# Projections, Fourier blocks and memory attention in phases, the later phases issued one unit behind

## The chip, the cores and the metric

The kernel runs on one core of a Trainium2 chip. The metric is the device time of one execution in microseconds; lower is better. The kernel before was timed three times: 2253.23, 2254.17 and 2257.09 us, median 2254.17.

The core has five engines, each with its own in-order instruction queue: TensorE (PE in the profile; PEld are its weight loads), VectorE (DVE), ScalarE (ACT), GpSimd (POOL) and SyncE (SP), which issues most of the DMAs. An engine waits on semaphores that the others raise.

## The reference

A two-layer encoder on a sequence of 1024 tokens of width 1024. In each layer, cut to the mixing part:

```python
h = _rmsnorm(x, g_pre_mix[l])
z = h @ w_in[l]
zf, zq, zk, zv, zm = jnp.split(z, splits, axis=-1)      # 256, 512, 128, 128, 256
y_f = _fourier_mix(zf, w_fourier[l])                    # FFT over tokens and channels, real part, then 64x64 maps
q, k = _rope(zq), _rope(zk)                             # 8 query heads, 2 key heads of 64
y_a = _window_attn(q, k, zv, sink[l])                   # keys within 128 tokens, one sink per head
y_m = _memory_attn(zm, km, vm)                          # 4 heads over 256 memory rows
y = concat([_rmsnorm(y_f), _rmsnorm(y_a), _rmsnorm(y_m)]) @ w_out[l]
x = x + _rmsnorm(y, g_post_mix[l])
```

A SwiGLU feed-forward block with width 2816 follows, again with a norm before and behind it. Everything is float32.

## The kernel before

Products run on TensorE in pairs of float32r halves: `split` (line 149) makes of an array a high half (an ACT cast, line 151) and the difference to it, the low half (line 152, on DVE, or on POOL where the caller says so). `Acc.add` (line 162) then issues three matmuls per block of 128 rows: high x high, high x low, low x high.

The 1024 tokens are eight tiles of 128. Per layer the mixing part does, in program order:

- `zf` (line 488): the projection for the Fourier group and its channel transform, by halves of the sequence; its results are the tiles `PQ`.
- `fourier_units` (line 509): one unit `even`, then four `e_out`, then `odd`, then four `o_out`. `even` and `odd` are long sums on DVE (line 512 in the profile). Each `e_out` and `o_out` ends in `finish`: load a table of cosines (`c_dft`), split it and the data, 6 products into a PSUM tile `yfp`, square and scale on ACT (lines 545 and 547, with a small POOL chain between), two transposes `yfT` on TensorE, two copies.
- `kvz` (line 625), one unit per token tile: 24 matmuls of 512 columns into `kvp` (keys, values, memory queries), then the readers of that PSUM tile: the split of the values, an ACT copy of the memory queries (line 639), and `rope` on the keys (DVE lines 612 and 614, then a POOL sum at line 617), then transposes `zT` (line 643) and `kT` (line 648) in the same unit.
- `q` (line 659): 24 matmuls into `qp`, `rope` (lines 612, 614, 617), four transposes `qT` (line 666), two stacks of halves. `q_load` fetches and splits the weights (eight 256 KB loads, `load_w512`, line 342, low halves on POOL). The weights of `kvz` and `q` share one pool of four buffers, `big`.
- `mem_units` (line 812): unit i does `mem_values` of pair i - 1 (transposes `mpT`, splits, products `mav`) and then `mem_scores` of pair i (products `ms`, maximum, exponential, scaling on POOL at line 790).
- `att_units` and `fm_units`: window attention and the output projection.

`weave` (line 59) merges two lists of units evenly in program order. The tile framework then decides the order on each engine from the program order, the dependences and its own timeline, so what runs next to what is read from the order lists below. PSUM has four pools of two banks: `sc`, `pT`, `av` and `pd` (line 42). `qp`, `qT` and `kvp` take `pd`; `kT` and `mav` take `av`. SBUF buffers are rings in two arenas (lines 125 to 136): a ring hands its places out in turn, and a place is written again only when its last reader is through.

## Time and profile before

| | |
|---|---|
| Median of three runs | 2254.17 us |
| The profiled execution's own time | 2256.81 us |
| Its span on the core, which the profile covers | 2255.0 us |
| Mean granted TensorE clock | 0.964 |
| TensorE busy | 2084.4 us |
| VectorE busy | 1495.7 us |
| ScalarE busy | 1078.5 us |
| GpSimd busy | 612.6 us |

A row of a table of stretches gives, for one stretch of the span, its length, the busy time of each engine with the number of instructions, the granted TensorE clock as a share of full speed, the mean busy share of the DMA engines and the rate. A row in order of time gives start, length, engine, line, operation, output<-input, shapes and count; in brackets stands how long the engine sat idle before it and which instruction it then waited for. The length of a row of several matmuls covers all of them. A row of a group gives the count, then busy time and mean of one in ns, then idle time before and its releasers.

### The profile page before, as it was taken

Reading aid. Unit: us, or ns where it says so; the run is one execution under the profiler, and the core shown is the slowest. Engines: PE = TensorE matmul, PEld = TensorE weight load, DVE = VectorE, ACT = ScalarE, POOL = GpSimd, SP = SyncE. Lnnn points to the kernel's source line nnn. Section 1 sums busy time; section 2 is a strip of 40 time slices with the busy share of each in tenths; the row PEclk is TensorE's granted clock in tenths of the full one; section 3 lists DMA queues with packets and bytes.
Section 4 is the critical chain, followed back from the end, with each engine's and each line's share of the span. In section 5 each row is a group of like instructions: output and inputs, shape, how many; then the busy total and the mean of one; then the engine's idle time right before and its main releaser. Section 6 shows DMA issues by size and latency. Waiting matters only on the chain.

```text
span 2255.0 us, 27659 instructions
## 1 busy us (share of the span) xinstructions
PE 2084.4 (92%) x9538; PEld 1703.3 (76%) x9538; DVE 1495.7 (66%) x2370; ACT 1078.5 (48%) x2179; POOL 612.6 (27%) x681
## 2 busy tenths in 40 slices
PE   7988898689999999999998789986999999999997
PEld 6767686568888887888886567765788888888876
DVE  7545878787676765565755478787867676644555
ACT  6354867553333334443544468675433333333343
POOL 5142425332222223210102334353522222200110
PEclk9989999889999999999998899998999999999999
DMA  6110322413222226666631112233222222255765
GB/s 212 33 54 2 101 86 84 140 47 103 75 94 75 94 71 197 220 194 209 221 117 33 40 43 75 76 122 112 75 76 93 75 94 75 91 182 169 239 206 177
DMA packets 135581, 252.85 MB, mean 112 GB/s; under 512 B 11256, under 2 KB 86032, under 8 KB 135440
## 3 DMA queue, kind: packets, MB, share of 16 engines
q1 hardware_dynamic: 129680, 240.59, 32.2%
q10 hardware_dynamic: 5760, 10.49, 1.2%
q8 instruction: 75, 1.23, 0.2%
q14 instruction: 66, 0.54, 0.1%
HBM read 201.76 MB, written 49.28 MB: 111 GB/s over the span
## 4 chain that ended last, share of the span: by engine, by line
PE 63%; DVE 6%; POOL 3%; issue 3%; ACT 3%; DMA 2%; DVEq 0%; SPq 0%; POOLq 0%; ACTq 0%
PE fo L1126 19%; PE qz L1026 10%; PE qx L1026 10%; PE qy L1026 10%; PE qw L1026 5%; PE mo L162 3%; DVE arena_r L152 2%; PE qp L162 2%; PE kvp L162 1%; PE zT L162 1%; POOL big L980 1%; DMA arena_f<-in_w_ffn_out 1%; DVE arena_f L1016 1%; ACT arena_r L151 1%; PE av L728 1%
## 5 line engine op out<-in xcount | busy, mean ns | idle before, releaser
L151 ACT CAST arena_r<-arena_f 128x512 fp32r<-128x512 f32 (+3 forms) x702 | 449.8, 660 | 774.4 <-PE fo L1126 181.6
L152 DVE TENSOR_TENSOR arena_r<-arena_f,arena_r 128x512 fp32r<-128x512 f32 (+4 forms) x678 | 571.6, 852 | 329.6 <-ACT arena_r L151 320.2
L1126 PE MATMUL fo<-arena_r 128*128 128x512 f32 x2112 | 491.4, 393 | 8.8 <-ACT arena_r L151 4.0
L1126 PEld LDWEIGHTS fo<-arena_r 128*128 128x128 f32 x2112 | 397.5, 189 | 95.6 <-ACT arena_r L151 5.9
L1026 PE MATMUL qy<-arena_r 128*128 128x512 f32 x1056 | 259.9, 396 | 15.6 <-ACT arena_r L151 9.6
L1026 PEld LDWEIGHTS qy<-arena_r 128*128 128x128 f32 x1056 | 201.4, 191 | 60.0 <-ACT arena_r L151 10.8
L1026 PE MATMUL qz<-arena_r 128*128 128x512 f32 x704 | 196.6, 390 | 4.5 <-ACT arena_r L151 1.9
L1016 DVE TENSOR_TENSOR arena_f<-arena_f 128x512 f32<-128x512 f32 x220 | 192.4, 878 | 11.2 <-DMA arena_f<-in_w_ffn_in 5.8
L1049 POOL TENSOR_TENSOR arena_f<-arena_f 128x512 f32<-128x512 f32 x44 | 76.0, 1728 | 423.0 <-ACT arena_f L1031 423.0
L1026 PEld LDWEIGHTS qz<-arena_r 128*128 128x128 f32 x704 | 132.1, 188 | 33.5 <-ACT arena_r L151 2.7
L1026 PE MATMUL qx<-big,arena_r 128*128 128x512 f32 x528 | 128.8, 393 | 2.5 <-DVE big L152 2.1
L208 POOL TENSOR_SCALAR rrsv<-rss 128x1 f32<-128x1 f32 x32 | 11.0, 342 | 442.2 <-ACT arena_f L320 225.7
L1026 PE MATMUL qw<-arena_r 128*128 128x512 f32 x528 | 129.1, 392 | 1.9 <-DVE arena_r L152 1.9
L1026 PE MATMUL qx<-arena_r 128*128 128x512 f32 x528 | 128.6, 393 | 1.7 <-DVE arena_r L152 1.7
L1078 POOL TENSOR_TENSOR arena_f<-arena_f 128x512 f32<-128x512 f32 x44 | 71.7, 1630 | 183.4 <-DVE arena_f L1059 104.5
L1026 PEld LDWEIGHTS qx<-big,arena_r 128*128 128x128 f32 x528 | 100.1, 190 | 24.6 <-DVE big L152 2.9
L1026 PEld LDWEIGHTS qx<-arena_r 128*128 128x128 f32 x528 | 100.4, 190 | 23.1 <-DVE arena_r L152 2.0
L1026 PEld LDWEIGHTS qw<-arena_r 128*128 128x128 f32 x528 | 99.8, 189 | 23.5 <-DVE arena_r L152 2.7
L1026 PE MATMUL qz<-big,arena_r 128*128 128x512 f32 x352 | 115.2, 389 | 0.0
L162 PE MATMUL qp<-big,arena_r 128*128 128x512 f32 x384 | 107.6, 433 | 3.1 <-POOL big L152 2.4
L162 PE MATMUL mo<-arena_r 128*128 128x512 f32 x384 | 105.0, 420 | 3.0 <-ACT arena_r L151 3.0
L162 PE MATMUL mo<-big,arena_r 128*128 128x512 f32 x384 | 101.1, 402 | 1.9 <-ACT arena_r L151 1.2
(197 smaller groups left out, 3225.5 us busy)
## 6 DMA issues: line engine op xcount, KB each, us to landing
arena_f<-in_w_ffn_out SPq DMA_DIRECT2D x132, 512.0 KB, 3.6
arena_f<-in_w_ffn_in SPq DMA_DIRECT2D x88, 512.0 KB, 3.5
actd<-arena_f SPq DMA_DIRECT2D x44, 512.0 KB, 2.6
arena_f<-actd SPq DMA_DIRECT2D x88, 192.0 KB, 2.8
arena_f<-in_w_in SPq DMA_DIRECT2D x40, 256.0 KB, 2.8
arena_f<-in_x SPq DMA_DIRECT2D x16, 512.0 KB, 4.3
arena_f<-in_w_out SPq DMA_DIRECT2D x32, 256.0 KB, 2.7
pmd<-arena_f ACTq DMA_DIRECT2D x32, 256.0 KB, 2.0
```

What stands on the lines that cost most here:

```text
L151: nc.scalar.copy(hi, src)
L152: return (lo_eng or nc.vector).tensor_tensor(out=lo, in0=src, in1=f32(hi), op=ALU.subtract)
L162: mm(self.dst, a, b, start=self.i == 0, stop=self.i == self.n - 1)
L208: nc.gpsimd.tensor_scalar(out=v, in0=ss, scalar1=1.0 / n, scalar2=EPS, op0=ALU.mult, op1=ALU.add)
L728: mm(av, lhs, p_, start=j == 0 and i == 0, stop=j == nk - 1 and i == 1)
L980: nc.gpsimd.tensor_tensor(out=b21, in0=b21, in1=b22, op=ALU.add)
L1016: nc.vector.tensor_tensor(out=s, in0=a, in1=b, op=op)
L1026: mm(pt, a, b, start=start and n == 0, stop=n == 11, skip_group_check=not start)
L1049: nc.gpsimd.tensor_tensor(out=self.v, in0=self.v, in1=self.s2, op=ALU.add)
L1078: (nc.gpsimd if i in (0, 3) else nc.vector).tensor_tensor(out=a[:, 512 * (i % 2) : 512 * (i % 2) + 512], in0=c, in1=g[i], op=ALU.mult)
L1126: mm(pts[t][m], a[:, x, sl], w[y][:, ns], start=ff == 0 and j == 0, stop=ff == NFF - 1 and j == 2)
```

## The change

- `finish` is cut into `halves` (table load and splits), `products` (the six products, square, scale) and `turned` (transposes and copies). Unit i does `halves` of block i, `products` of block i - 1, `turned` of block i - 2. `odd` moves into unit 1.
- `kvz` first copies the whole PSUM tile to SBUF with one ACT instruction (ring `kvs` of three); values, `rope` and memory queries read that copy, and the values' low half is made on POOL. Its transposes become `kvz_turn`, called one unit behind by the new helper `skewed`.
- `q` keeps products and `rope`; the transposes become `q_turn`, one unit behind, and `qT` moves from the PSUM pool `pd` to `av`. The ring for query `rope` has six places instead of four, elsewhere in the arena.
- `mem_values` is cut into `mem_turn` (transposes and splits) and `mem_values` (products); unit i does scores of pair i, values of pair i - 2, transposes of pair i - 1.
- `load_w512` makes low halves in turn on DVE and POOL instead of on POOL alone. The ring `tabs` has four places instead of two.
- `q_load` stands before the last unit of `kvz_turn`; `fm_load` moves into the weave of the memory units, after the last query products.

```diff
-    ropes = {2: run(6, 4, 0.5), 8: run(8, 4, 2)}
+    ropes = {2: run(6, 4, 0.5), 8: run(36, 6, 2)}
...
-            split(hi, lo, raw, nc.gpsimd)
+            split(hi, lo, raw, (nc.vector, nc.gpsimd)[k % 2])
...
+            order = (0, 4, 2, 6, 1, 5, 3, 7)
+
+            def unit(i):
+                if i == 1:
+                    odd()
+                if i < 8:
+                    (e_out if order[i] % 2 == 0 else o_out)(order[i])
+                if 1 <= i < 9:
+                    products(order[i - 1])
+                if i >= 2:
+                    turned(order[i - 2])
+
+            return [even] + [lambda i=i: unit(i) for i in range(10)]
...
             wmov(self.wkvz, self.hT, t, pt)
+            r = kvs(512)
+            nc.scalar.copy(r, pt)
             vst = self.vst[half][:, c]
-            split(vst[:, :, 0, :], vst[:, :, 1, :], pt[:, P : 2 * P].rearrange("p (g d) -> p g d", g=2))
-            z = zs_(256)
-            nc.scalar.copy(z, pt[:, 2 * P : 4 * P])
-            kr = self.rope(pt[:, 0:P], 2, t)
+            split(vst[:, :, 0, :], vst[:, :, 1, :], r[:, P : 2 * P].rearrange("p (g d) -> p g d", g=2), nc.gpsimd)
+            self.kvr[t] = self.rope(r[:, 0:P], 2, t), r[:, 2 * P : 4 * P]
+
+        def kvz_turn(self, t):
+            half, c = divmod(t, 4)
+            kr, z = self.kvr.pop(t)
             zt = ps([2, P], "zT", "pT")
...
+        def skewed(self, f, g, n):
+            def unit(t):
+                if t < n:
+                    f(t)
+                if t:
+                    g(t - 1)
+            return [lambda t=t: unit(t) for t in range(n + 1)]
...
-            qr = self.rope(pt, 8, t).rearrange("p h d -> p (h d)")
-            qt = ps([4, P], "qT")
+            self.qr[t] = self.rope(pt, 8, t).rearrange("p h d -> p (h d)")
+
+        def q_turn(self, t):
+            half, c = divmod(t, 4)
+            qr = self.qr.pop(t)
+            qt = ps([4, P], "qT", "av")
...
             def unit(i):
-                if i >= SKEW:
-                    h, half = todo[i - SKEW]
+                if i < n:
+                    st[i] = self.mem_scores(*todo[i])
+                if i >= 2:
+                    h, half = todo[i - 2]
...
-                    self.mem_values(h, half, st.pop(i - SKEW))
-                if i < len(todo):
-                    st[i] = self.mem_scores(*todo[i])
+                    self.mem_values(h, half, pp.pop(i - 2))
+                if 1 <= i <= n:
+                    pp[i - 1] = self.mem_turn(st.pop(i - 1))
...
-        weave(mix.fourier_units(), tiles(mix.kvz) + [mix.q_load])
-        for t in range(4):
-            mix.q(t)
+        kvz = mix.skewed(mix.kvz, mix.kvz_turn, NT)
+        weave(mix.fourier_units(), kvz[:8] + [mix.q_load] + kvz[8:])
+        q = mix.skewed(mix.q, mix.q_turn, NT)
+        for u in q[:4]:
+            u()
         mem.load()
-        weave(mix.mem_units(), tiles(mix.q)[4:])
+        weave(mix.mem_units(), q[4:8] + [mix.fm_load] + q[8:])
         fm = mix.fm_units(pmd)
-        weave(mix.att_units(0), [mix.fm_load] + fm[:6] + [mix.out_load] + fm[6:])
+        weave(mix.att_units(0), fm[:6] + [mix.out_load] + fm[6:])
```

The order on TensorE in layer 0 at the query tiles, before: `qp` are a tile's products, `qT` its four transposes, `ms` memory scores. The tile whose transposes are `qT_1348` has its products (`qp_1320`) ahead of these rows.

```order
L550 MATMUL yfT_1315<-const,arena_f 128x128 x2
L666 MATMUL qT_1348<-const,arena_f 128x128 x4
L162 MATMUL qp_1357<-big_1266,arena_r 128x512 x6
L162 MATMUL qp_1357<-big_1273,arena_r 128x512 x6
L162 MATMUL qp_1357<-big_1280,arena_r 128x512 x6
L162 MATMUL qp_1357<-big_1287,arena_r 128x512 x6
L778 MATMUL ms_1501<-arena_r 128x256
L778 MATMUL ms_1510<-arena_r 128x256
L666 MATMUL qT_1385<-const,arena_f 128x128 x4
L162 MATMUL qp_1394<-big_1266,arena_r 128x512 x6
```

The same place after, from the end of the second tile (`qp_1348`) on; `qT_1376` belongs to the first tile (`qp_1320`), `qT_1413` to the second.

```order
L162 MATMUL qp_1348<-big_1273,arena_r 128x512 x6
L547 MATMUL yfT_1294<-const,arena_f 128x128 x2
L815 MATMUL ms_1492<-arena_r 128x256
L815 MATMUL ms_1501<-arena_r 128x256
L162 MATMUL qp_1385<-big_1252,arena_r 128x512 x6
L162 MATMUL qp_1385<-big_1259,arena_r 128x512 x6
L162 MATMUL qp_1385<-big_1266,arena_r 128x512 x5
L703 MATMUL qT_1376<-const,arena_f 128x128 x2
L666 MATMUL zT_1299<-const,arena_f 128x128 x2
L547 MATMUL yfT_1315<-const,arena_f 128x128 x2
L703 MATMUL qT_1376<-const,arena_f 128x128 x2
L162 MATMUL qp_1385<-big_1266,arena_r 128x512
```

Before, a tile's transposes stood directly behind its products; now they stand most of a tile or more later, and the first two tiles are interleaved while their weights arrive.

The second place is TensorE in layer 1 between the last products of the Fourier projection (`pq_8913`) and the first Fourier products (`yfp`). Before:

```order
L162 MATMUL pq_8913<-arena_r 128x256 x6
L643 MATMUL zT_8986<-const,arena_f 128x128 x2
L162 MATMUL kvp_9222<-big_8921,arena_r 128x512 x6
L162 MATMUL kvp_9222<-big_8928,arena_r 128x512 x6
L162 MATMUL kvp_9222<-big_8935,arena_r 128x512 x6
L162 MATMUL kvp_9222<-big_8942,arena_r 128x512
L648 MATMUL kT_8993<-const,arena_f 128x128
L162 MATMUL kvp_9222<-big_8942,arena_r 128x512 x5
L162 MATMUL yfp_9001<-arena_r 128x256
```

After, the rows that follow the same products (a further kvz tile, `kvp_9192`, has moved ahead of them):

```order
L162 MATMUL pq_8913<-arena_r 128x256 x6
L666 MATMUL zT_9023<-const,arena_f 128x128 x2
L666 MATMUL zT_9093<-const,arena_f 128x128 x2
L162 MATMUL kvp_9264<-big_8921,arena_r 128x512 x6
L162 MATMUL kvp_9264<-big_8928,arena_r 128x512 x6
L162 MATMUL kvp_9264<-big_8935,arena_r 128x512 x6
L162 MATMUL kvp_9264<-big_8942,arena_r 128x512 x6
L162 MATMUL kvp_9329<-big_8921,arena_r 128x512 x6
L162 MATMUL kvp_9329<-big_8928,arena_r 128x512 x2
L671 MATMUL kT_9030<-const,arena_f 128x128
```

The rest of `kvp_9329` follows, and then the first `yfp`: one kvz tile stood between the two places before, two stand there now.

The third place is VectorE in layer 1 around the long sums of `even` (line 512, 1024 columns). Before, with `kvp` as the input of the keys' `rope` (lines 612 and 614):

```order
L152 TENSOR_TENSOR arena_r<-kvp_9149,arena_r 128x2x64
L512 TENSOR_TENSOR arena_f<-arena_f 128x1024 x4
L387 TENSOR_TENSOR arena_r<-zT_8986,arena_r 64x2x128
L612 TENSOR_TENSOR arena_f<-kvp_9084,const 128x128
L614 TENSOR_TENSOR arena_f<-kvp_9084,const 128x128
L512 TENSOR_TENSOR arena_f<-arena_f 128x1024 x2
```

After (`rope` is lines 631 and 633 there):

```order
L152 TENSOR_TENSOR arena_r<-zT_8862,arena_r 128x512
L512 TENSOR_TENSOR arena_f<-arena_f 128x1024 x4
L387 TENSOR_TENSOR arena_r<-zT_9023,arena_r 64x2x128
L631 TENSOR_TENSOR arena_f<-arena_f,const 128x128
L633 TENSOR_TENSOR arena_f<-arena_f,const 128x128
L387 TENSOR_TENSOR arena_r<-zT_9093,arena_r 64x2x128
L512 TENSOR_TENSOR arena_f<-arena_f 128x1024
```

The products of `rope` still stand behind the first four sums, but they read the copy in SBUF; no VectorE instruction reads `kvp` any more.

More of the change, by code (lines that the diff above doesn't have):

```diff
@@ L598, in o_out @@
                     STT(d[:, 1], O[1][:, 1, 0], s, O[1][:, 0, 1])
[L599 to L602 removed]
+                halves(r, d)
+            order = (0, 4, 2, 6, 1, 5, 3, 7)
[9 more added lines that the diff above has]
+            return [even] + [lambda i=i: unit(i) for i in range(10)]
         def rope(self, src, n, t):
@@ L793, in mem_scores, with mem_turn @@
             return e
-        def mem_values(self, h, half, e):
-            av = ps([512], "mav", "av")
+        def mem_turn(self, e):
+            res = []
             for mt in range(2):
@@ L801, in mem_values @@
                 pp = mps(2, 512, dt=F32R)
-                ph, pl = pp[:, 0], pp[:, 1]
-                split(ph, pl, pT.rearrange("p h q -> p (h q)"))
+                split(pp[:, 0], pp[:, 1], pT.rearrange("p h q -> p (h q)"))
+                res.append((pp[:, 0], pp[:, 1]))
+            return res
+        def mem_values(self, h, half, pp):
+            av = ps([512], "mav", "av")
+            for mt in range(2):
                 lhs = self.mem.vm[:, mt, h].rearrange("p a d -> p (a d)")
-                for i, p_ in enumerate((ph, pl)):
-                    mm(av, lhs, p_, start=mt == 0 and i == 0, stop=mt == 1 and i == 1)
+                for i in range(2):
+                    mm(av, lhs, pp[mt][i], start=mt == 0 and i == 0, stop=mt == 1 and i == 1)
             s = h % 2
```

43 lines of the change are left out of this document (23 added, 20 removed).

## The prediction

> **What bounds the kernel now.** I read the page first (its busy times), then a table of stretches, then TensorE's order of time inside the stretches that the change touches.
>
> ```profile
> PE 2084.4 (92%) x9538; PEld 1703.3 (76%) x9538; DVE 1495.7 (66%) x2370; ACT 1078.5 (48%) x2179; POOL 612.6 (27%) x681
> ```
>
> TensorE (PE) is the bound: 92% busy, while VectorE (DVE) has 66%. So only PE's idle time and its slow-clock time can be won. The edited stages lie at 75 to 260 us (layer 0) and 1200 to 1369 us (layer 1). Columns: stretch, its length, busy time of PE, PEld, DVE, ACT, POOL, each with its count, then granted clock, DMA share, GB/s.
>
> ```profile
> 75.00:135.05 60.05, 57.80 (x292) 47.83 (x291) 37.06 (x75) 28.52 (x80) 17.17 (x28) 1.00 0.11 32
> 135.05:194.74 59.69, 45.10 (x169) 33.91 (x168) 21.63 (x42) 23.26 (x58) 17.60 (x21) 0.80 0.13 37
> 194.74:260.35 65.61, 54.69 (x281) 41.25 (x279) 56.43 (x122) 47.43 (x126) 22.85 (x37) 0.97 0.18 57
> 1200.31:1303.49 103.18, 79.88 (x364) 63.76 (x363) 55.80 (x109) 49.34 (x130) 34.71 (x45) 0.87 0.14 40
> 1303.49:1368.90 65.41, 53.89 (x281) 40.19 (x279) 56.51 (x122) 47.42 (x126) 23.04 (x37) 1.00 0.17 53
> ```
>
> Three kinds of stretch stand here. From 75 to 135 PE is full at clock 1.00: nothing to win. The second and the fourth row have a paused PE and a low clock with no other engine near full: the room is here. In the third and fifth row (memory attention) DVE works 56 of 65 us, so PE's gaps there are not free for the taking.
>
> **How much room.** Issue intervals at full clock, from runs without a pause (start, length, instruction, count):
>
> ```profile
> 82.15 5.18 PE L162 MATMUL kvp<-big,arena_r 128*128 128x512 f32 x22
> 119.03 1.67 PE L162 MATMUL yfp<-arena_r 128*128 128x256 f32 x12
> 194.57 1.03 PE L800 MATMUL mpT<-const,arena_f 128*128 128x128 f32 x8
> ```
>
> One matmul lasts 0.39 us for 512 columns (0.28 and 0.27 for the others), the rest of the length is intervals: (5.18 - 0.39)/21 = 0.228 us, (1.67 - 0.28)/11 = 0.126, (1.03 - 0.27)/7 = 0.108. The counts of q and kvz products, by stretch (135 to 195, then 1200 to 1303.5):
>
> ```profile
> L162 PE MATMUL qp<-big,arena_r 128*128 128x512 f32 x120 | 38.7, 483 | 1.8 <-POOL big L152 1.7
> ```
>
> ```profile
> L162 PE MATMUL qp<-big,arena_r 128*128 128x512 f32 x120 | 32.9, 427 | 1.3 <-POOL big L152 0.7 <-DVE arena_f L614 0.4 <-ACT big L151 0.3
> L162 PE MATMUL kvp<-big,arena_r 128*128 128x512 f32 x112 | 27.9, 399 | 0.3 <-DVE arena_f L614 0.3
> L162 PE MATMUL yfp<-arena_r 128*128 128x256 f32 x48 | 10.4, 366 | 3.4 <-ACT arena_r L151 2.8 <-DVE arena_r L152 0.6
> ```
>
> Layer 0, 169 instructions: 120 x 0.228 + 49 others at about 0.11 = 27.4 + 5.4 = 32.8 us of work in 59.7, **slack 26.9**. Layer 1, 364 instructions: 232 x 0.228 + 48 x 0.126 + 84 others at 0.117 = 52.9 + 6.0 + 9.8 = 68.7 in 103.2, **slack 34.5**.
>
> **The change, part by part.**
>
> *Query tiles.* PE stands between the products of a tile and its transposes. First the sum over both layers (us, times, longest), then rows in order of time, the first and last of four tiles in each layer and the longest pause:
>
> ```profile
> PE qT L666 <- POOL arena_f L617: 21.5, 10, 2.9
> ```
>
> ```profile
> 154.93 8.12 PE L162 MATMUL qp<-big,arena_r 128*128 128x512 f32 x24
> 176.38 0.66 PE L666 MATMUL qT<-const,arena_f 128*128 128x128 f32 x4 [2.88 <-POOL arena_f L617]
> 187.53 7.21 PE L162 MATMUL qp<-big,arena_r 128*128 128x512 f32 x24
> ```
>
> ```profile
> 1267.28 6.68 PE L162 MATMUL qp<-big,arena_r 128*128 128x512 f32 x24
> 1297.77 5.72 PE L162 MATMUL qp<-big,arena_r 128*128 128x512 f32 x24
> ```
>
> It waits 21.5 us, for the rotation (two DVE products, one POOL sum). The new order puts the next tile's products there: one tile is 0.39 + 23 x 0.228 = 5.6 us, twice the longest wait, so the wait goes and nothing new is late behind it. The tile also takes 7 to 8 us instead of 5.6, since the clock is down after each pause:
>
> ```profile
> 150.00:155.00 5.00, 1.53 (x7) 1.13 (x7) 1.29 (x2) 1.10 (x3) 1.29 (x2) 0.50 0.01 3
> 160.00:165.00 5.00, 3.28 (x15) 2.52 (x14) 1.29 (x2) 0.81 (x2) 0.55 (x1) 1.00 0.00 0
> ```
>
> The clock is half in one stretch and full 10 us later. Over 5.6 each, the four tiles lose 7.5 us to it in layer 0 (8.12 to 7.21, 30.0 together) and 3.3 in layer 1 (6.68 to 5.72, 25.8 together): about 10.7 us. Both losses are inside the slack. I take the clock to follow the pauses.
>
> [...]
>
> *Query weights.* PE also waits for the split weights, made by POOL alone; DVE's price for such a difference stands in the last row:
>
> ```profile
> 143.48 2.52 POOL L152 TENSOR_TENSOR big<-arena_f,big 128x512 fp32r<-128x512 f32 x2 [0.69 <-ACT big L151]
> 142.84 1.57 PE L162 MATMUL qp<-big,arena_r 128*128 128x512 f32 x3 [0.77 <-POOL big L152]
> ```
>
> ```profile
> L152 POOL TENSOR_TENSOR big<-arena_f,big 128x512 fp32r<-128x512 f32 x7 | 8.9, 1283 | 1.6 <-ACT big L151 1.6
> ```
>
> ```profile
> L152 DVE TENSOR_TENSOR arena_r<-arena_f,arena_r 128x512 fp32r<-128x512 f32 x8 | 6.0, 756 | 1.4 <-ACT arena_r L151 1.4
> ```
>
> Eight differences cost 10.3 us on POOL; four on each cost 5.1 and 3.0. The weights end at 146.0 now; even one after the other (8.1 us) they end some 2 us earlier, unless the loads set it; I take 145. More counts the order: PE works two tiles at once while the weights arrive. Walk: the 10 us until 145 hold 34 of the two tiles' 48 products (7.8 us) and a few small ones; by the order the other 14 (3.2 us) follow, tile 1 ends at 148; three more tiles (72 x 0.228 = 16.4) with about 3 us of transposes and scores end at 168 against 194.7. That uses all the slack; for waits of the in-order queues on splits, copies and banks I keep 4 us. **Layer 0: -23.**
>
> *Keys, values, Fourier in layer 1.* DVE has the long sums of the Fourier step in its queue and the kvz tile's rotation stands behind them, holding the PSUM bank:
>
> ```profile
> 1206.00:1230.00 24.00, 14.94 (x65) 11.96 (x64) 21.50 (x40) 10.51 (x31) 8.39 (x10) 0.72 0.11 33
> 1205.86 4.63 DVE L512 TENSOR_TENSOR arena_f<-arena_f 128x1024 f32<-128x1024 f32 x4 [1.11 <-ACT arena_f L507]
> 1211.38 3.95 DVE L512 TENSOR_TENSOR arena_f<-arena_f 128x1024 f32<-128x1024 f32 x6
> 1217.22 1.18 PE L162 MATMUL yfp<-arena_r 128*128 128x256 f32 x2 [2.76 <-ACT arena_r L151]
> 1225.04 0.69 PE L550 MATMUL yfT<-const,arena_f 128*128 128x128 f32 x2 [3.56 <-ACT arena_f L547]
> ```
>
> PE issues 65 instructions in 24 us at clock 0.72. After, one ACT copy frees the bank, and the order has three and a half kvz tiles (88 x 0.228 = 20 us) before the first Fourier products: PE can run to about 1224 while DVE finishes its sums. What follows is 24 + 120 products of 512 columns, 48 Fourier ones and some 50 small ones, 45 us, so 1270 at best. But DVE has its 55.8 us, plus 3 for the weights, to do between 1206 and there, over 90% full; at 83%, a little under its 86% in memory attention (56.4 of 65.6), it ends near 1276. **Layer 1: -27** (1303.5 to 1276), of the slack of 34.5.
>
> *What is added.* Per kvz tile ACT copies 512 columns instead of 256: about 0.59 for 0.37 us, 0.2 x 8 per layer, beside ACT's 23 of 60 busy. If that cover were gone it would cost 1.8 per layer. The copy's ring of three is freed only by an earlier tile's rotation and transposes, a wait that the trace lacks. Behind the waiting copy stand ACT's Fourier casts, and PE's next kvz tile but one waits for the bank. It costs nothing if PE has done the transposes, and up to a tile's 5.6 us once per layer if not; inside the friction I kept. Four more differences per layer lie on DVE before the first kvz tile: 0 to 3 us each layer, taken as 0. The rotation's DVE products now read SBUF twice instead of PSUM and SBUF. Such an operation has been seen to stall beside POOL (DVE 0.43 us alone):
>
> ```profile
> 205.50 1.26 POOL L617 TENSOR_TENSOR arena_f<-arena_f 128x512 f32<-128x512 f32 x1 [2.53 <-PE mpT L800]
> 205.84 1.20 DVE L152 TENSOR_TENSOR arena_r<-arena_f,arena_r 128x256 fp32r<-128x256 f32 x1
> 213.97 0.43 DVE L152 TENSOR_TENSOR arena_r<-arena_f,arena_r 128x256 fp32r<-128x256 f32 x1
> ```
>
> [...]
>
> So 32 products may each lose 0 to 0.8 us of DVE, 25 at the worst; POOL is busy a third of the time, and DVE is not the bound where most stand: 0 on the path, 6 at the upper end. *Memory attention* is cut into three phases; DVE's 56.4 us per layer stay, so I leave its 65.6 and 65.4 us as they are. Its two parts now are:
>
> ```profile
> 195.00:225.00 30.00, 27.88 (x153) 22.45 (x151) 22.63 (x45) 18.31 (x51) 11.47 (x18) 1.00 0.01 1
> 225.00:260.00 35.00, 26.55 (x129) 18.53 (x127) 33.64 (x78) 28.77 (x75) 11.04 (x19) 0.95 0.33 105
> ```
>
> DVE is 75% busy in the first and 96% in the second. All at 95% it would give 6 per layer (56.4/0.95 = 59.4), all at 75% lose 10.
>
> The first 60 us of layer 0, with PE at 57.8 of 60, gain nothing: there the change does not do what it says. Output weights are asked for earlier in the program, but their buffers are the query weights', free only after the last query tile; in SP's queue the eight query-weight loads only change places with one Fourier table (128 KB).
>
> **Sum.** The profiled execution took 2256.8 us. 2256.8 - 23 - 27 = 2206.8. The median of the three runs before, 2254.2, is 2.6 lower, so I predict **2205**.
>
> **Rivals.**
> 1. *Memory attention gives half back.* Query tiles end sooner, the memory units start one phase later, and a chain of waits holds DVE at 75%: 56.4/0.75 = 75 us instead of 65.5, +10 per layer, with some 3 more from stalled rotations: 2228. For it: more memory units are left after the last query tile. Against: DVE runs at 96% in the second part now. Chance 0.14.
> 2. *The clock stays low*, whatever the pauses: +10.7, 2216. Against it: clock 1.00 from 75 to 135. Chance 0.11.
> 3. *More than I take*: all the slack (61.4) and 6 per layer in memory attention: 2254 - 73 = 2181. Chance 0.08.
> 4. *Slower.* Query transposes move to the two PSUM banks that the memory values use. Now a value group holds its bank from its first product until its sum is read, a transpose from its first piece until its second difference:
>
> ```profile
> 196.40 1.11 PE L806 MATMUL mav<-arena_r 128*128 128x512 f32 x3
> 197.64 0.66 PE L666 MATMUL qT<-const,arena_f 128*128 128x128 f32 x4
> ```
>
> ```profile
> 201.38 0.69 DVE L387 TENSOR_TENSOR arena_r<-qT,arena_r 64x512 fp32r<-64x512 f32 x1 [0.36 <-ACT arena_r L386]
> 203.29 0.68 DVE L810 TENSOR_TENSOR arena_f<-mav,arena_f 64x512 f32<-64x512 f32 x1 [1.22 <-ACT arena_f L809]
> ```
>
> That is 7.6 us (to 203.97) and 4.4 (to 202.07): 12 us of two banks, 6 per pair, against 8.2 per unit now (65.6/8). It decides only once a pair holds its banks above 8.2 + 3.1 = 11.3 us (what eats 50 us over 16 pairs), twice the 6; at 12 the time is 2265. Chance 0.04.
> 5. *Gains and losses cancel*, within 0.2% (about what a measurement tells from no change here): 2254. Chance 0.03.
>
> The forecast, 2194 to 2216, keeps 0.60. Range: from rival 3's neighbourhood to rival 1's, **2184 to 2230**. Faster by over 0.2%: 0.60 + 0.14 + 0.11 + 0.08 = 0.93; same 0.03; slower 0.04.
>
> **What would show it.** Right: no wait of query transposes for POOL over 1 us; four query tiles of about 5.6 us each; clock at 0.95 or above in the query stretches; the layer 1 stretch from the first kvz product after 1200 to the fifth query tile near 76 us. Wrong: a memory stretch above 70 us with PE waiting for DVE or for a bank; kvz products waiting for ACT's copy; Fourier products late in layer 1 because DVE is full.

## The result, and the profile after

| | before | after |
|---|---|---|
| Median, timed together | 2253.7 us (2252.24 to 2257.09) | 2200.76 us (2199.33 to 2201.17) |
| The profiled execution's own time | 2256.81 us | 2200.58 us |
| Its span | 2255.0 us | 2198.8 us |

The ratio is 0.9762, 95% interval 0.9745 to 0.9779: faster by 53 us, where 49 (2254.2 to 2205) were forecast.

The page of the changed kernel, busy times of its engines:

```profile
PE 2058.4 (94%) x9538; PEld 1692.4 (77%) x9538; DVE 1501.1 (68%) x2370; ACT 1078.3 (49%) x2179; POOL 602.6 (27%) x681
```

PE has the same 9538 instructions. It is busy for 26 us less, because fewer of them ran at the low clock (mean granted clock 0.973 for 0.964), and it is idle for 30 us less. Next, stretches of the changed kernel, then the answering ones of the kernel before that the prediction did not show (columns as in the prediction's stretches). They run from the first product of the key tiles to the end of the fifth query tile (layer 0), from there to the first transpose of window attention (memory attention), the same two of layer 1, and last the window attention of layer 0.

```profile
74.16:163.10 88.94, 87.16 (x446) 73.15 (x445) 59.26 (x109) 48.62 (x124) 33.36 (x47) 1.00 0.16 47
163.10:228.93 65.83, 57.64 (x286) 44.88 (x284) 56.68 (x127) 50.58 (x135) 25.89 (x43) 0.89 0.18 57
1164.88:1244.90 80.02, 72.66 (x359) 59.62 (x358) 56.40 (x102) 44.94 (x117) 28.30 (x40) 0.96 0.17 51
1244.90:1311.81 66.91, 56.27 (x285) 44.14 (x283) 57.12 (x126) 51.91 (x138) 23.52 (x40) 0.92 0.17 52
228.93:417.79 188.86, 162.09 (x833) 133.20 (x833) 144.16 (x347) 126.51 (x324) 77.55 (x132) 0.95 0.30 106
```

```profile
77.07:194.74 117.67, 100.83 (x451) 80.05 (x450) 58.00 (x116) 50.92 (x135) 34.03 (x47) 0.90 0.12 35
260.35:452.96 192.61, 166.74 (x833) 136.47 (x833) 144.61 (x347) 127.86 (x322) 78.07 (x134) 0.93 0.30 104
```

In layer 0 the stretch from the key tiles to the fifth query tile falls from 117.67 to 88.94 us, its clock rises from 0.90 to 1.00, and PE is now busy in 87 of 89 us. In layer 1 the answering stretch of 103.18 us becomes 80.02. Memory attention stays as long as it was: 65.61 and 65.83, 65.41 and 66.91. Its clock is lower now (0.89 and 0.92 for 0.97 and 1.00): PE has run ahead and waits for DVE, which is busy 56.68 of 65.83 us.

The query tiles of layer 0 in PE's order of time, changed kernel (start, length, instruction, count; a bracket would show a wait):

```profile
150.42 0.60 PE L703 MATMUL qT<-const,arena_f 128*128 128x128 f32 x4
150.77 7.08 PE L162 MATMUL qp<-big,arena_r 128*128 128x512 f32 x30
...
157.81 0.60 PE L703 MATMUL qT<-const,arena_f 128*128 128x128 f32 x4
...
158.84 5.18 PE L162 MATMUL qp<-big,arena_r 128*128 128x512 f32 x22
```

No transposes wait any more, and 30 products take 7.08 us: an interval of (7.08 - 0.39)/29 = 0.231 us, full clock. By stretches, from PE's order of time of both kernels (us; layer 1 counted from its first key product, 1165.6 before and 1130.2 after):

| stretch | before | after | difference |
|---|---|---|---|
| start to first key product | 77.1 | 74.2 | -2.9 |
| keys to fifth query tile, layer 0 | 117.7 | 88.9 | -28.8 |
| memory attention, layer 0 | 65.6 | 65.8 | +0.2 |
| window attention, layer 0 | 192.6 | 188.9 | -3.7 |
| up to layer 1's first key product | 712.6 | 712.4 | -0.2 |
| keys to fifth query tile, layer 1 | 137.9 | 114.7 | -23.2 |
| memory attention, layer 1 | 65.4 | 67.0 | +1.6 |
| window attention, layer 1 | 187.3 | 187.6 | +0.3 |
| the rest | 698.8 | 699.4 | +0.6 |

### The profile page after: what moved, and what is told of

Same layout as the page of the kernel before. It is cut to its first block, busy times and chain, and to the rows that moved or that the text cites. A ratio compares the mean times of both kernels' runs of the same rounds, so it can differ in the third digit from the quotient of the medians.

```text
span 2198.8 us, 27667 instructions
## 1 busy us (share of the span) xinstructions
PE 2058.4 (94%) x9538; PEld 1692.4 (77%) x9538; DVE 1501.1 (68%) x2370; ACT 1078.3 (49%) x2179; POOL 602.6 (27%) x681
## 4 chain that ended last, share of the span: by engine, by line
PE 74%; DVE 9%; ACT 6%; POOL 4%; issue 3%; DMA 3%; SPq 0%; DVEq 0%; ACTq 0%; POOLq 0%
PE fo L1171 19%; PE qz L1071 10%; PE qy L1071 10%; PE qx L1071 10%; PE mo L162 5%; PE qw L1071 5%; DVE arena_r L152 3%; PE qp L162 3%; PE kvp L162 3%; PE zT L162 2%; PE av L765 1%; PE pT L758 1%; ACT arena_r L151 1%; PE sc L721 1%; DMA arena_f<-in_w_ffn_out 1%
## 5 line engine op out<-in xcount | busy, mean ns | idle before, releaser
L151 ACT CAST arena_r<-arena_f 128x512 fp32r<-128x512 f32 (+4 forms) x718 | 453.9, 652 | 753.2 <-PE fo L1171 187.9
L152 DVE TENSOR_TENSOR arena_r<-arena_f,arena_r 128x512 fp32r<-128x512 f32 (+4 forms) x678 | 565.7, 843 | 335.9 <-ACT arena_r L151 328.1
L1071 PEld LDWEIGHTS qx<-arena_r 128*128 128x128 f32 x528 | 100.9, 191 | 23.2 <-DVE arena_r L152 2.0
L162 PE MATMUL mo<-arena_r 128*128 128x512 f32 x384 | 99.5, 407 | 5.5 <-ACT arena_r L151 3.2
L162 PE MATMUL qp<-big,arena_r 128*128 128x512 f32 x384 | 98.0, 398 | 1.0 <-DVE arena_f L633 0.5
```

The source lines that it names most:

```text
L151: nc.scalar.copy(hi, src)
L152: return (lo_eng or nc.vector).tensor_tensor(out=lo, in0=src, in1=f32(hi), op=ALU.subtract)
L162: mm(self.dst, a, b, start=self.i == 0, stop=self.i == self.n - 1)
L1071: mm(pt, a, b, start=start and n == 0, stop=n == 11, skip_group_check=not start)
```

## The experiments

Twelve kernels ran, each timed against the kernel before on the same chip (its medians there: 2253.3 to 2255.3 us). Where a run is compared with the changed kernel, that is 2200.76 us, measured where the kernel before took 2253.7. Times of a run are medians of four to six executions; stretches, waits and rows come from one profiled execution of it. The executions of one kernel spread by 2 to 8 us, so a difference of a few us in one stretch is no more than a hint.

### The query tiles: the order or the bank?

The change does two things to them. The transposes stand one unit behind in the program, and their PSUM tile moves from `pd`, the two banks of the products, to `av`. The prediction gave the gain to the order and saw in the bank only a danger. But the framework decides the order on the engine itself, among what banks and buffers allow. So each half was undone alone in the changed kernel, and made alone in the kernel before.

```diff
-        q = mix.skewed(mix.q, mix.q_turn, NT)
+        q = tiles(lambda t: (mix.q(t), mix.q_turn(t)))
```

> The changed kernel with the query tiles in one unit again: the transposes of a tile stand directly behind its own products and rotation in the program, as before; their PSUM tile keeps its new banks, those of the memory values. Theory 1 (the order in the program, one unit behind, took the pauses away): the waits of the query transposes for POOL come back, about 21 us in ten, and the low clock behind them, about 10 us; 2225 to 2233 us. Theory 2 (the bank did it: before, products and transposes of the queries shared two banks, so the products of the tile after next had none; with banks of their own the framework itself issues the next products ahead of the transposes): no such wait over 1 us, 2198 to 2205 us.

Measured 2200.69 us, ratio 0.9757 (0.9743 to 0.9772): the same as the changed kernel. Nothing waits for POOL at the query transposes. Its order of time in layer 0:

```profile
153.67 0.60 PE L703 MATMUL qT<-const,arena_f 128*128 128x128 f32 x4
154.02 8.22 PE L162 MATMUL qp<-big,arena_r 128*128 128x512 f32 x35
```

The program says tile by tile; the engine has products of the next tiles between a tile's products and its transposes all the same (35 in a row, where a tile has 24).

```diff
-            qt = ps([4, P], "qT", "av")
+            qt = ps([4, P], "qT")
```

> The changed kernel with the query transposes back in the two PSUM banks of the query products, everything else as changed, so the transposes stay one unit behind in the program. Theory 1 (order): no change beyond noise, 2198 to 2204 us, since the next tile's products still stand ahead of the transposes. Theory 2 (bank): the products of every second tile wait for the rotation of the tile before to read its bank (two DVE products, some 1.4 us) and for the transposes' own bank, 1 to 2 us in each of 14 tiles with low clock behind some: 2212 to 2230 us, with query products waiting for DVE.

Measured 2213.51 us, ratio 0.9818 (0.98 to 0.9835), inside the range of theory 2, but not for its reason. The query stretches are as in the changed kernel (89.6 and 114.5 us for 88.9 and 114.7); the transposes wait for POOL 4.7 us in four in all. Its span is 9.9 us longer (2208.7), and that is lost elsewhere: 3.5 us in the memory attention of layer 0, 1.8 and 5.8 in the two window attentions. So the order, too, is enough to remove most of the pauses (4.7 us of 21.5 are left) while the rest of the change is there.

```diff
-            qt = ps([4, P], "qT")
+            qt = ps([4, P], "qT", "av")
```

> The kernel before with one edit of the change alone: the query transposes get the PSUM banks of the memory values; order in the program, weights, copies and memory attention as before. Theory 1 (order): nothing gained, 2250 to 2258 us. Theory 2 (bank): the pauses of the query tiles (21.5 us) and part of the low clock (10.7 us) go, 2222 to 2235 us; the first 145 us and the layer 1 stretch up to the first query tile stay as before.

Measured 2219.11 us, ratio 0.9846 (0.9829 to 0.9864): this one word in the kernel before brings 36 us, two thirds of the whole change. The stretches from the keys to the fifth query tile fall by 21.6 us in layer 0 (117.7 to 96.1) and 17.7 in layer 1 (137.9 to 120.2), and no query transpose waits. These two stretches hold the whole gain: the span is 39 us shorter.

```profile
153.86 8.90 PE L162 MATMUL qp<-big,arena_r 128*128 128x512 f32 x31
162.59 1.03 PE L666 MATMUL qT<-const,arena_f 128*128 128x128 f32 x8
163.38 4.13 PE L162 MATMUL qp<-big,arena_r 128*128 128x512 f32 x17
```

The transposes of two tiles now come together, after the products of both.

```diff
-            qr = self.rope(pt, 8, t).rearrange("p h d -> p (h d)")
-            qt = ps([4, P], "qT")
+            self.qr[t] = self.rope(pt, 8, t).rearrange("p h d -> p (h d)")
+
+        def q_turn(self, t):
+            half, c = divmod(t, 4)
+            qr = self.qr.pop(t)
+            qt = ps([4, P], "qT")
...
-            mix.q(t)
+        q = mix.skewed(mix.q, mix.q_turn, NT)
```

> The kernel before with the other half of the query edit alone: the transposes of a query tile one unit behind its products in the program, both still in the same two PSUM banks. Theory 1 (order or bank, either is enough, as each was when the other was undone in the changed kernel): the waits of query transposes for POOL go, the query tiles take 5.7 us, 2217 to 2230 us, near the 2219 of the bank alone. Theory 2 (in the kernel before the shared banks still hold the products of the next tile, and only the other edits of the change hid that): waits of query products for DVE take the place of those of the transposes, 2238 to 2254 us.

Measured 2229.65 us, ratio 0.9882 (0.9866 to 0.9898): 26 us. It lies at the edge of theory 1's range. The two stretches fall to 99.7 and 127.4 us (17.9 and 10.5 less), and the memory attention of layer 0 gets 4.6 longer. Of the waits (21.5 us in ten) this is left:

```profile
PE qT L680 <- POOL arena_f L617: 9.2, 4, 3.1
```

So either edit removes pauses, and the bank removes all of them. That the bank gives the framework the freedom to reorder is how I read the order lists; the runs show the new order and the gain. The two do not add up (36 and 26 alone, 53 with everything else). A kernel with all the rest of the change and neither of the two was not run.

### The clock: does it follow the pauses?

The prediction put 10.7 us on the low clock behind the pauses. Here the rotation stays as it was, but PE gets something to do while it runs. The added products are placed behind the tile's last product, and the transposes behind the added products:

```diff
+            if t < 4:
+                dum = ps([512], "fill", "sc")
+                with tc.issue_after(last["mm"].ins):
+                    for i in range(9):
+                        mm(dum, hsl(self.hT, half, 0, 0, slice(c * P, c * P + P)), self.wq[0][0], start=i == 0, stop=i == 8)
```

> The kernel before with nine more products of 512 columns between the products of a query tile and its transposes, in the first four tiles of each layer, written to a spare PSUM bank that nobody reads (extra work, about 0.23 us each at full clock, 2.2 us per tile, as long as the mean wait there). It removes no wait: the transposes still come after the rotation. Theory 1 (the low clock follows the pauses): the clock stays at 1.00 through these tiles, each takes 5.6 us instead of 8.1 to 5.7, and the program gets 6 to 11 us faster although it does more: 2243 to 2248 us. Theory 2 (the clock is low for another reason, a window of its own or the load of the other engines): the tiles keep 7 to 8 us, the added products take time at the low clock, 2254 to 2266 us.

Measured 2247.42 us, ratio 0.9964 (0.9952 to 0.9976): 8 us faster (5 to 11 by the interval) with 72 more products. Layer 0 in order of time:

```profile
155.28 1.12 PE L675 MATMUL qT<-const,arena_f 128*128 128x128 f32 x4 [2.88 <-POOL arena_f L620]
156.04 7.64 PE L150 MATMUL qp<-big,arena_r 128*128 128x512 f32 x24
163.52 2.20 PE L150 MATMUL fill<-big,arena_r 128*128 128x512 f32 x9
166.41 0.66 PE L675 MATMUL qT<-const,arena_f 128*128 128x128 f32 x4 [0.69 <-POOL arena_f L620]
166.83 5.73 PE L150 MATMUL qp<-big,arena_r 128*128 128x512 f32 x24
```

The first tile shows the control: its added products came too early, a pause of 2.88 us stayed, and its 24 products took 7.64 us. Where the added products cover the pause to 0.69 us, and to 0.85 in the tile after these rows, the next 24 take 5.73 and 5.71. In these tiles the clock follows the pauses: shown. How much of the 8 us is this, is less sure. The layer 0 stretch falls by 4.2 us (117.7 to 113.5), the layer 1 stretch by 0.5, where the first tile, again after a pause of 2.88, takes 8.10 us for 6.68. The window attentions are 4.5 and 2.5 us shorter, of which more below, and other parts together 4 longer.

### Weights, Fourier blocks, key tiles, memory attention

Four parts of the change were undone one by one in the changed kernel, and the copy of the key tile as a fifth. The longer rings (`tabs`, `ropes`) and the places of `q_load` and `fm_load` were not undone by themselves.

```diff
-            split(hi, lo, raw, (nc.vector, nc.gpsimd)[k % 2])
+            split(hi, lo, raw, nc.gpsimd)
```

> The changed kernel with the low halves of the key, value and query weights on POOL alone again. Theory 1 (the arrival of the weights orders the work): the first kvz product comes at 76 to 77 us instead of 74.2, query products wait for POOL's halves again as they did before (2.4 us in all), the stretch up to the fifth query tile of layer 0 gets 3 to 6 us longer, layer 1 the same 1 to 4: 2206 to 2212 us. Theory 2 (POOL keeps up, since the loads set the pace): only the first 75 us change, 2200 to 2204 us.

Measured 2219.6 us, ratio 0.9841 (0.9826 to 0.9855): 19 us slower than the changed kernel, more than theory 1 had. The first key product comes at 77.3 us, as in the kernel before; the layer 0 stretch grows by 6.3 us (88.9 to 95.3), with waits of 4.3 us in a row and a clock of 0.66 from 150 to 160 us:

```profile
146.66 0.41 PE L666 MATMUL zT<-const,arena_f 128*128 128x128 f32 x2 [1.17 <-DVE arena_r L387]
148.63 0.38 PE L815 MATMUL ms<-arena_r 128*128 128x256 f32 x1 [1.57 <-ACT arena_f L540]
149.66 0.41 PE L547 MATMUL yfT<-const,arena_f 128*128 128x128 f32 x2 [0.65 <-DVE arena_r L380]
150.98 8.59 PE L162 MATMUL qp<-big,arena_r 128*128 128x512 f32 x24 [0.91 <-DVE arena_f L633]
```

The last low half of layer 0's query weights is ready at 143.5 us, in the changed kernel at 137.9. Layer 1's stretch grows by 1.8. Another 9.2 us come from the two window attentions (+5.9 and +3.3), whose instructions do not read these weights.

```diff
             def unit(i):
-                if i == 1:
-                    odd()
-                if i < 8:
-                    (e_out if order[i] % 2 == 0 else o_out)(order[i])
-                if 1 <= i < 9:
-                    products(order[i - 1])
-                if i >= 2:
-                    turned(order[i - 2])
+                (e_out if order[i] % 2 == 0 else o_out)(order[i])
+                products(order[i])
+                turned(order[i])
...
```

> The changed kernel with each Fourier block in one unit again (sums, halves, products, transposes in a row, the long odd sums in a unit of their own after the fourth block). Theory 1 (cutting the blocks took the waits of products and transposes away): the waits of Fourier products and transposes, 11.6 us in both layers before and 5.4 after, come back, with low clock behind some: 2206 to 2214 us, lost in the stretches from the first kvz product to the fifth query tile. Theory 2 (the framework moves the pieces itself once banks and buffers allow it, as it did with the query tiles): 2198 to 2203 us.

Measured 2208.49 us, ratio 0.9801 (0.9787 to 0.9816): 7.7 us slower, theory 1, and where it said: the layer 1 stretch is 121.1 us for 114.7. Its one long new wait there is that of the first Fourier products, 7.9 us, for an ACT cast that itself waits for the long sums on DVE; the changed kernel has 1.3. First this kernel, then the changed one, the waits of PE of 1 us and more in that stretch (sum, times, longest):

```profile
PE yfp L162 <- ACT arena_r L151: 7.9, 1, 7.9
PE yfT L547 <- ACT arena_f L540: 3.6, 1, 3.6
PE qp L162 <- DVE arena_f L629: 1.8, 1, 1.8
```

```profile
PE yfT L547 <- ACT arena_f L540: 3.4, 1, 3.4
PE yfp L162 <- DVE arena_r L152: 1.3, 1, 1.3
PE kvp L162 <- ACT arena_f L656: 1.0, 1, 1.0
```

Layer 0 shows no difference (88.2 us for 88.9). The rest nearly cancels: 1.9 and 2.7 us less in the window attentions, 5.7 more behind the second.

```diff
-        kvz = mix.skewed(mix.kvz, mix.kvz_turn, NT)
+        kvz = tiles(lambda t: (mix.kvz(t), mix.kvz_turn(t)))
```

> The changed kernel with the transposes of a kvz tile in the same unit as its products again; the copy to SBUF stays. Theory 1 (order): the next tile's products wait for rotation and copy, 1 to 2 us in most of the 14 tiles, with low clock: 2208 to 2225 us. Theory 2 (buffers: the copy frees the bank of the products at once, and the transposes have other banks, so the framework can issue the next products first): 2198 to 2204 us.

Measured 2218.48 us, ratio 0.9846 (0.9831 to 0.986): in theory 1's range, and yet theory 1 is wrong. The stretches that hold the key tiles are 90.2 and 114.9 us for 88.9 and 114.7: next to nothing. Of the 16.6 us by which its span is longer, 12.1 are lost in the window attention of layer 0 (201.0 us for 188.9), which begins a whole memory attention later. What happens there is below.

```diff
-            r = kvs(512)
-            nc.scalar.copy(r, pt)
+            z = kvs(256)
+            nc.scalar.copy(z, pt[:, 2 * P : 4 * P])
             vst = self.vst[half][:, c]
-            split(vst[:, :, 0, :], vst[:, :, 1, :], r[:, P : 2 * P].rearrange("p (g d) -> p g d", g=2), nc.gpsimd)
-            self.kvr[t] = self.rope(r[:, 0:P], 2, t), r[:, 2 * P : 4 * P]
+            split(vst[:, :, 0, :], vst[:, :, 1, :], pt[:, P : 2 * P].rearrange("p (g d) -> p g d", g=2))
+            self.kvr[t] = self.rope(pt[:, 0:P], 2, t), z
```

> The changed kernel without the copy of the whole kvz tile: values, rotation and memory queries are read from PSUM as before (an ACT copy of 256 columns, the values' low half on DVE), and the transposes stay one unit behind. Theory 1 (the copy is what gains in layer 1, since DVE holds the bank behind the long Fourier sums): the waits of kvz products for DVE come back, the stretch of layer 1 from the first kvz product to the fifth query tile grows from 114 us by 10 to 20; layer 0 by 0 to 5: 2210 to 2225 us. Theory 2 (the copy is not needed once order and query banks are free): 2198 to 2204 us.

Measured 2201.05 us, ratio 0.977 (0.9754 to 0.9787): the same as the changed kernel. In the total the copy to SBUF brings nothing; without it the layer 0 stretch is 2.0 us longer (91.0 for 88.9), and other stages are shorter. One wait of key products for the rotation does come back:

```profile
1185.68 6.36 PE L162 MATMUL kvp<-big,arena_r 128*128 128x512 f32 x20 [3.89 <-DVE arena_f L633]
```

But the layer 1 stretch is 113.8 us for 114.7: the time is won back before its end. The wait takes the place of others: PE waits 6.9 us in that stretch in all, with the copy 7.2.

```diff
-                if i < n:
-                    st[i] = self.mem_scores(*todo[i])
-                if i >= 2:
+                if i >= 1:
...
-                    self.mem_values(h, half, pp.pop(i - 2))
-                if 1 <= i <= n:
-                    pp[i - 1] = self.mem_turn(st.pop(i - 1))
+                    self.mem_values(h, half, self.mem_turn(st.pop(i - 1)))
+                if i < n:
+                    st[i] = self.mem_scores(*todo[i])
```

> The changed kernel with memory attention in two phases again (values with their transposes of the pair before, then scores). Theory 1 (DVE, over 90% busy in the last 40 us of memory attention, sets its length, whatever the phases): 2197 to 2204 us, memory stretches 66 and 67 us as with three phases. Theory 2 (three phases saved waits which the earlier query tiles would have brought): PE waits for the memory transposes' scaling and halves grow by 5 us per layer or more, 2207 to 2215 us.

Measured 2208.95 us, ratio 0.9804 (0.9789 to 0.9819). For memory attention itself theory 1 holds: 67.5 and 63.9 us together 131.4, with three phases 132.8. The 8 us of the total are lost elsewhere: 4.2 in the window attention of layer 0, 2.2 in the feed-forward part behind it, 4.9 behind the window attention of layer 1, less 1.6 in that window attention itself and the 1.4 of memory attention. Theory 2 has the total right and the place wrong.

### A stage that no edit touches

The window attention (with the output projection woven into it) and what follows that of layer 1 have the same code in all these kernels, except in the new versions below. Their lengths (us):

| kernel | window attention, layer 0 | layer 1 | behind it |
|---|---|---|---|
| before | 192.6 | 187.3 | 698.8 |
| after | 188.9 | 187.6 | 699.4 |
| queries in one unit | 187.4 | 183.2 | 702.7 |
| query bank as before | 190.7 | 193.4 | 700.6 |
| before with the bank | 190.1 | 185.8 | 699.1 |
| before with the order | 192.6 | 184.2 | 698.9 |
| before with added products | 188.1 | 184.8 | 700.8 |
| low halves on POOL | 194.8 | 190.9 | 699.1 |
| Fourier in one unit | 187.0 | 184.9 | 705.1 |
| key tiles in one unit | 201.0 | 189.3 | 703.0 |
| no copy | 192.2 | 187.9 | 698.5 |
| memory in two phases | 193.1 | 186.0 | 704.3 |

The last column spreads by 7 us over some 700, window attention by 14 and 10 over some 190. Part of this may be the spread of one kernel from run to run. But the order of window attention on PE is not the same either: the framework lays out the whole program along its own timeline, so an edit shifts the choices in stages that it doesn't touch. Of the 818 instructions that PE issues in layer 0 from the first transpose of window attention to the feed-forward part, 569 stand in the same sequence in the changed kernel and in the one with key tiles in one unit, when they are matched by name without the tiles' numbers. PE's order list at one place in this stage, the changed kernel above, the other below (the first number counts the rows of the list; `mo` is the output projection, `sc` scores, `av` values):

```
379 L162 MATMUL mo_2443<-big_2010,arena_r 128x512 x3
380 L162 MATMUL mo_2443<-big_2017,arena_r 128x512 x3
381 L721 MATMUL sc_2634<-arena_r 128x384 x2
382 L765 MATMUL av_2377<-arena_r 128x512
383 L721 MATMUL sc_2638<-arena_r 128x384 x2
```

```
376 L765 MATMUL av_2377<-arena_r 128x512
377 L721 MATMUL sc_2634<-arena_r 128x384 x2
378 L721 MATMUL sc_2638<-arena_r 128x384 x2
379 L765 MATMUL av_2377<-arena_r 128x512
```

Below the second list the projection `mo_2443` follows only after four transposes. The stretch of the kernel with key tiles in one unit answers to the fifth row of the changed kernel above:

```profile
233.60:434.60 201.00, 170.91 (x832) 138.54 (x832) 145.87 (x347) 125.98 (x321) 75.35 (x134) 0.91 0.28 100
```

The same work takes PE 171 us instead of 162 (clock 0.91 for 0.95), and it is idle for 30 us instead of 27. That the order differs is shown; which of its differences costs the 12 us was not tried (all four executions of this kernel lie 17 to 20 us above the changed one's median, so the loss is no single run's), and neither was a kernel with the order of this stage held fixed.

### New versions

In the end of memory attention DVE is 92% busy and PE waits; here the changed kernel, layer 0, and the first 80 us of window attention behind it:

```profile
188.00:228.93 40.93, 32.74 (x147) 23.71 (x145) 37.71 (x89) 34.09 (x90) 16.48 (x28) 0.83 0.25 80
228.93:308.93 80.00, 80.00 (x420) 68.05 (x421) 58.76 (x179) 56.84 (x155) 27.68 (x51) 0.98 0.27 93
```

Two versions move its last units into window attention:

```diff
-        weave(mix.mem_units(), q[4:8] + [mix.fm_load] + q[8:])
+        m = mix.mem_units()
+        weave(m[:6], q[4:8] + [mix.fm_load] + q[8:])
...
-        weave(mix.att_units(0), fm[:6] + [mix.out_load] + fm[6:])
+        weave(mix.att_units(0), m[6:] + fm[:6] + [mix.out_load] + fm[6:])
```

> A new version: the changed kernel with the last four of the ten memory units taken out of the weave with the query tiles and woven into window attention instead. Theory 1 (the end of memory attention is bound by DVE, 92% busy from 188 to 229 us, while the window attention behind it has DVE at 72%; spreading the work lets PE run on): memory stretch and window attention together lose 4 to 8 us per layer, 2186 to 2195 us. Theory 2 (PE is over 97% busy in the first 80 us of window attention, and what is put there only moves, or the framework's order gets worse): 2197 to 2208 us.

Measured 2210.65 us, ratio 0.98 (0.9785 to 0.9814): 10 us slower than the changed kernel. (In this version rings of the arena meant for stages apart overlap, the memory scores and the projection's squares and sums, both at places 16 to 23, so its memory scores are not the reference's; its instructions are the same ones.) Memory attention falls to 58.1 and 61.4 us, 13.3 less together, and window attention grows to 201.6 and 193.2, 18.3 more. Theory 2: the work only moves. PE has no room there (80.00 busy of 80.00 us, last row above); whether the framework's order got worse as well was not taken apart.

> The same new version with only the last two memory units woven into window attention. Theory 1: half of the gain, 2192 to 2198 us. Theory 2: 2197 to 2206 us.

Measured 2208.29 us, ratio 0.9786 (0.977 to 0.9803). Memory attention 63.9 and 68.0, window attention 189.3 and 193.7: a little slower than either theory had, and no gain. No version here beats the changed kernel.

## Why the prediction was right, and where it was not

- **The bound.** PE's idle and slow-clock time was what could be won, in the two stretches named: 28.8 + 23.2 = 52 of the 56 us between the two profiled executions. Right.
- **Query tiles.** "The wait goes and nothing new is late behind it": right; no query transpose waits, and the tiles run at full clock (1.00 from 74.16 to 163.10 us and from 1201.50 to 1244.90). The reason given, the new order, is only half of it. The bank alone removes all the waits, and the order can be undone without loss. The prediction had read the order list as if the program had put it there; it is the framework that chose. With the old order of the program the two shared banks kept it from choosing better; with the new one it finds nearly as good an order in them. The change made both edits together, so the forecast came out although the prediction credited the gain to one alone.
- **The clock follows the pauses**, 10.7 us: shown by the added products. The tiles they covered lost nothing (24 products in 5.73 and 5.71 us), the one they missed lost as before (7.64). The runs do not agree with rival 2, which rested on the clock staying low. The 0.50 from 150 to 155 us, which the prediction put down to a pause of a query tile, is not its work: the clock was 0.50 from 149.78 us on, and that pause of 2.88 us began at 151.3. Ahead of the fall PE was busy for 1.83 of 3.42 us (from 146.36 to 149.78), and a pause of 1.98 us, ahead of `yfT`, had begun at 148.6. Nor is the clock down after each pause: the last section has one of 2.17 us with 0.50 behind it, and one of the same length with 1.00.
- **Layer 0, -23.** It was -28.8. The size is off. The weights come sooner than was taken: 145 us for their last low half, and it is ready at 137.94 (2.9 us of the difference because the whole stretch begins sooner):

```profile
136.65 1.29 POOL L152 TENSOR_TENSOR big<-arena_f,big 128x512 fp32r<-128x512 f32 x1
```

So PE does not wait for weights, and of the 4 us kept for waits of the in-order queues 1.8 were paid in the whole stretch, by one instruction. With these 1.8 us left in it, the slack gives 25.1 of the 28.8. Of the other 3.7, about 0.4 are the transposes of the fourth tile, which now stand behind the stretch, and 2.2 are waits ahead of 135 us that are gone (`kvp` for DVE, 1.7, and `zT` for ACT, 0.5), where "the first 60 us of layer 0 gain nothing" stood. The remaining 1 us stays open: the slack itself is an estimate from counts.
- **Query weights.** That two tiles could be worked as the weights arrive was right, and the split over two engines carries it: 6.3 us of this stretch are lost when it is undone, and the weights are then ready 5.6 us later.
- **Layer 1, -27.** It was -23.2 (103.2 to 80.0 us, where 76 were expected), and its reason was mostly wrong. The step "one ACT copy frees the bank" failed: without the copy the stretch is no longer. "At 83%" DVE was to set the end; it is busy 56.4 of 80.0 us, 70%. What gained were the query tiles (17.7 by the bank alone or 10.5 by the order alone, in the kernel before) and the cut Fourier blocks (6.4, in the changed kernel); that the two add up in one kernel was not tried. PE comes to the first Fourier products 24.3 us into this stretch, as worked out (1224 against 1200.3). The 4 us by which the end is late lie in what the sum had at nothing: the chain of the first Fourier block, waits of 1.3 and 3.4 us, with the clock at half for 6.8 us from within the second on.
- **What is added.** ACT's copy cost 1.0 us of PE once, in layer 1, inside the friction kept. The rotation from SBUF did not stall: the median product on 128x128 takes 0.29 us as it did from PSUM, the longest 0.55. "Four more differences on DVE before the first kvz tile: 0 to 3 us, taken as 0" had the wrong sign: -2.9. A store of the memory values stands in SP's queue behind three loads of Fourier tables, and these wait for low halves of the key weights, which two engines now make. The three loads and the copy that waits for the store, kernel before, then changed:

```profile
50.70 6.48 SPq L534 DMA_DIRECT2D arena_f<-c_dft  x3
...
60.39 1.07 ACT L507 COPY arena_f<-pq 128x512 f32<-128x512 f32 x2 [3.25 <-DMA kvd<-arena_f]
```

```profile
51.05 4.43 SPq L558 DMA_DIRECT2D arena_f<-c_dft  x3
...
58.68 1.07 ACT L507 COPY arena_f<-pq 128x512 f32<-128x512 f32 x2 [1.45 <-DMA kvd<-arena_f]
```

The store leaves right behind them, at 55.58 us instead of 57.23, and the copy that waited for it and PE behind it follow. The rest is clock: 0.50 from 61.0 to 67.9 us before, 1.00 there after. With the halves on POOL again the store went at 57.25 and the first key product came at 77.3.
- **Memory attention unchanged.** Right: +0.2 and +1.6. Two phases or three make no difference there. That DVE's 56 us set its length is only in part so: with the same work for DVE it took from 60.5 us (layer 1 without the copy) to 70.2 (layer 1 with the queries in one unit).
- **Window attention** was not in the sum: -3.7 in layer 0. Errors of both signs stand against each other in the total: layer 0 -5.8, prologue -2.9 and this one against layer 1 +3.8 and memory attention +1.8; they leave the 6 us between the expected 50 and the 56 of the two profiled executions. So the total is nearer than its parts, and that is luck.
- **Rivals.** Memory attention gave nothing back; the clock did not stay low; the new bank of the query transposes, the one that was to make it slower, is by itself enough for the main gain. Giving the old bank back to the changed kernel costs 13 us, but of these 0.7 at most lie in the stretches with the query tiles.

## What to carry to other kernels

Where a framework orders the engine, ask first which bank or buffer forbids the better order: one tile moved to another PSUM pool brought two thirds of what the whole rewrite did. A pause of PE cost its length here and sometimes the clock after it (24 products took 7.21 us behind one pause of 2.17 us, 5.72 behind another), so price both. And compare such kernels by stretches: undoing one edit moved up to 12 us in a stage with no edited line, and three of these runs have a theory's total for a reason that is not the theory's.

## What was not expected of the hardware

Some pauses well below 3 us had a low clock behind them, and in these traces their length alone does not say which. In the kernel before, two query transposes wait 2.17 us each, one in layer 0 and one in layer 1. Each with the 24 products behind it, and a third one of 2.49 us between them:

```profile
187.01 0.86 PE L666 MATMUL qT<-const,arena_f 128*128 128x128 f32 x4 [2.17 <-POOL arena_f L617]
187.53 7.21 PE L162 MATMUL qp<-big,arena_r 128*128 128x512 f32 x24
...
1276.68 1.11 PE L666 MATMUL qT<-const,arena_f 128*128 128x128 f32 x4 [2.49 <-POOL arena_f L617]
...
1297.36 0.66 PE L666 MATMUL qT<-const,arena_f 128*128 128x128 f32 x4 [2.17 <-POOL arena_f L617]
1297.77 5.72 PE L162 MATMUL qp<-big,arena_r 128*128 128x512 f32 x24
```

After the first pause of 2.17 us the products take 7.21 us, after the second 5.72, full clock. The granted clock (start:end, length, PE busy, clock, DMA share, GB/s), first around the pause of layer 0, then around that of layer 1:

```profile
183.91:187.32 3.41, 1.24 (x10) 1.00 0.00 0
187.32:190.74 3.42, 3.42 (x12) 0.50 0.00 0
```

```profile
1293.24:1296.66 3.42, 1.94 (x12) 1.00 0.00 0
1296.66:1300.07 3.41, 2.71 (x14) 1.00 0.00 0
```

The first pause lies whole in the row at 1.00, which is idle for 2.17 us, and the next row has 0.50. Around the second PE is idle for 1.48 us in one row and 0.70 in the next, and the clock is 1.00 in both. Which pauses bring the clock down, and what sets the moment, is not shown by any run here. Shorter pauses in a row had a low clock behind them in the kernel with low halves on POOL (above: 1.57, 0.65 and 0.91 us, then a clock of 0.66 from 150 to 160 us). Behind a longer one, in the first of the two new versions, the products kept nearly the pace of full clock: PE waits 3.11 us from 1462.4 us on, and the ten products of 512 columns from 1468.62 us on take 2.66 us, 0.25 us apart, where an interval at full clock is 0.23.

At the pause of 2.49 us the clock falls ahead of the transposes: it is 1.00 up to 1276.18 us and 0.50 from there to 1279.59, and the transposes begin at 1276.68.
